# An einsum of attention weights and values: v through SyncE's queue in float32 with a cast on VectorE, and stores of four heads by SyncE

## The chip, the core and the metric

The kernel runs on one core of one Trainium2 chip. The core has TensorE (PE: matrix products, and transposes as products with an identity), VectorE (DVE), ScalarE (ACT), GpSimd (POOL) and SyncE (SP), each with its own instruction stream, and 16 DMA engines that move data between HBM and the core's on-chip memory (SBUF). DMAs issued by POOL stand in one queue (q0 in the profile), those issued by SP in another (q1); all 16 DMA engines serve both. Engines order themselves by semaphores: an instruction or a finished DMA raises one, another waits until it has reached a count; a DMA raises its semaphore by 16 in all. The metric is the device time of one execution in microseconds; lower is better.

## The reference

```python
attn_weights: (8, 12, 1024, 1024) float32
v:            (8, 12, 1024, 64)   float32
out = einsum('bhqs,bhsd->bhqd', attn_weights, v)      # float32
```

So there are 96 independent heads, and for each a product of a 1024x1024 matrix with a 1024x64 matrix. The weights are 402.7 MB, v and the output 25.2 MB each.

## The kernel before

**Tiling.** Four consecutive heads make a quad (`VH = 4`, `NV = 24` quads, called q). A quad is worked off in two units (`NU = 48` units, called n, so q = n // 2). The 128 partitions hold four heads by 32 blocks of rows. A unit takes 16 of the 32 rows of each block: `load_attn(n)` brings them as one DMA from POOL, cast by the DMA from float32 to bfloat16, into one of two buffers `abf[n % 2]` (64 KB read and 32 KB written for each partition). The last two units are loaded in two halves (`HALVED`).

**PE, one unit** (`pe_unit`). It waits for the load, transposes 16 groups g (four instructions each, line 132) into four PSUM banks in turn, from which DVE (10 groups) and ACT (6 groups) copy them to `at` (line 256, `copy_g`). In the first unit of a quad it then spreads v (line 147): v arrives as `vr`, two quads wide, in the layout of the DMA, and a product with a 0/1 matrix brings it to the partitions where the product needs it; DVE and ACT copy the result to `vbf` (line 232). Then it transposes the result of the unit before back (line 159), ACT copies that to the output buffer `osb` (line 239, `back_copies`), and PE multiplies (line 174). DVE and ACT each copy half of the product to `ot` (line 268, `product`), which releases the back transposes of the next unit.

**POOL** issues nearly all DMAs, in one written order. After the transposes of unit n (it waits for DVE's groups, `s_t[True]`) it issues load n + 2. In the first unit of an odd quad it first waits until the spread of that quad is done (`s_sp`) and issues the load of v for the next two quads (`load_v`, line 325): one DMA of 2 MB, cast by the DMA into `vr`. In the first unit of an even quad, after the load, it stores two finished quads (`store_2`, line 332, 2 MB). From quad 16 (`HELD_FROM`) on stores are held: quads 16 to 19 are stored by POOL after the last load, quads 20 to 23 by SP at the end.

**SP** loads the first two quads of v at the start, as float32, into `v32` (the last two slots of `osb`, which only the last two quads use for output), in four DMAs (line 385); DVE casts them to `vr` in one instruction (line 309). Then SP is a relay: it waits for each load in turn (line 396) and raises `s_half`, for which PE waits ahead of group 8; when a load of v has landed it raises `s_vr`, for which PE waits ahead of the spread; when a store has landed it raises `s_free`, for which ACT waits before it writes that slot of `osb` again. At load 35 it issues 15 tiny DMAs to `small`, a buffer that nothing reads (line 400): the k-th has k rows of k + 1 elements.

**Output slots.** `slot(q)` is q % 4 for quads 0 to 17, so four slots go round, and one slot each for the later quads.

Of the kernel before, what the change touches and what calls it, by code (L numbers as in the profile page):

```python
# [10 lines left out]
def kernel(  # L11
# [18 lines left out]
    nc = tc.nc  # L30
# [8 lines left out]
    VH = 4  # L39
    VP = P // VH  # L40
# [6 lines left out]
    NV = NH // VH  # L47
    NU = 2 * NV


    HELD_FROM = NV - 8
    BY_SYNC = NV - 4


    LOOPED = HELD_FROM
    NO = 8 + 2
    SMALL_AT = (33,)

    HALVED = NU - 2

    def slot(q):
# [4 lines left out]
    out_2 = out.rearrange("b h q d -> (b h) q d").rearrange(  # L66
        "(hq two four) (p r) d -> hq (four p) two (r d)", two=2, four=VH, p=VP
    )
    v_2 = v.rearrange("b h q d -> (b h) q d").rearrange(
        "(hq two four) (p r) d -> hq (four p) two (r d)", two=2, four=VH, p=VP  # L70
    )

    def on_dve(g):
        return g % 8 in (0, 2, 4, 5, 7)
# [8 lines left out]
    with tc.tile_critical(no_gpsimd_drain=True):  # L83
        sem = tc.alloc_semaphore
        sb = lambda name, shape, dt: nc.alloc_sbuf_tensor(name, shape, dt).ap()
        ident = sb("ident", [P, P], fp32)
# [5 lines left out]
        ot = sb("ot", [P, GH, P], fp32)  # L92
        osb = sb("osb", [P, NO, 2 * G, D], fp32)

        v32 = osb[:, ds(NO - 2, 2)].rearrange("p n r d -> p (n r d)")
        small = sb("small", [16, 2, 16, 16], fp32)
        bank = [nc.alloc_psum_tensor(f"bank{i}", [P, 512], fp32).ap() for i in range(8)]
        pt = [b.rearrange("p (k j) -> p k j", k=KW) for b in bank[:4]]
# [3 lines left out]

        s_abf = [sem(f"s_abf{i}") for i in range(2)]
        s_second = {n: sem(f"s_second{n}") for n in range(HALVED, NU)}
        s_v0, s_v = sem("s_v0"), sem("s_v")
        s_osb = [sem(f"s_osb{i}") for i in range(2)]
        s_held, s_end, s_small = sem("s_held"), sem("s_end"), sem("s_small")

        s_t = {True: sem("s_t_dve"), False: sem("s_t_act")}
# [114 lines left out]
        def engine(dve):  # L224
            eng = nc.vector if dve else nc.scalar
            copy = nc.vector.tensor_copy if dve else nc.scalar.copy
            per = PER_DVE if dve else PER_ACT
            e = 0 if dve else 1

            def spread_copy(h, ps, count):  # L230
                eng.wait_ge(s_sp[e], count)
                copy(  # L232
                    out=vbf[:, :, h], in_=ps.rearrange("p (k d) -> p k d", k=SB)
                ).then_inc(s_vbf[e])

            def back_copy(rows, j0, jn, ps, count):

                eng.wait_ge(s_back, count)
                return copy(  # L239
                    out=rows.rearrange("p (half j) d -> p j half d", half=2)[:, ds(j0, jn)],  # L240
                    in_=ps[:, ds(0, jn * P)].rearrange("p (j half d) -> p j half d", half=2, d=D),
                )

            def rows_of(n):
                return osb[:, slot(n // 2), ds(n % 2 * G, G)]

            def back_copies(rows, count, free=None):
                if free is not None:
                    eng.wait_ge(s_free, free)
                for k in range(2):  # L250
                    last = back_copy(rows, 4 * k, 4, px[k], count + k + 1)
                last.then_inc(s_out)

            def copy_g(g, count):
                eng.wait_ge(s_t[dve], count)  # L255
                ins = copy(  # L256
                    out=at[:, g].rearrange("c k j two -> c (k j two)"),
                    in_=bank[g % 4].bitcast(bf16),
                )
                if g < G - 4:  # L260
                    ins.then_inc(s_cp[g])
                elif g == (G - 1 if dve else G - 2):
                    ins.then_inc(s_last[e])

            def product(count):

                eng.wait_ge(s_m[e], count)
                copy(  # L268
                    out=ot.rearrange("c j (h p) -> c h j p", h=VH)[:, ds(2 * e, 2)],
                    in_=po[e].rearrange("c (h j p) -> c h j p", h=2, j=GH),  # L270
                ).then_inc(s_ot[e])

            mine = [g for g in range(G) if on_dve(g) == dve]

            def unit(n, base, rows, free):

                of_t, of_sp, of_back, of_m = base
                for g in mine:
                    copy_g(g, of_t + (n * per + count_of(g)))
                if n % 2 == 0:  # L280
                    spread_copy(e, po[e], of_sp + (n + 1))
                    spread_copy(2 + e, px[e], of_sp + (n + 2))
                if not dve:
                    back_copies(rows, of_back + 2 * n, free)
                product(of_m + (n + 1))


            un, iters = (2, NV) if dve else (8, LOOPED // 4)
            with nc.Fori(1, iters + 1, 1, engines=(DVE if dve else ACT,)) as it:  # L289
                base = [eng.snap(it * (un * k) - un * k) for k in (per, 1, 2, 1)]  # L290
                of_free = None if dve else eng.snap(it * 2 - 1)
                for n in range(un):
                    rows = osb[:, (n - 1) // 2 % 4, ds((n - 1) % 2 * G, G)]

                    free = of_free + n // 4 if n in (1, 5) and not dve else None
                    unit(n, base, rows, free)
            for n in range(un * iters, NU):
                free = LOOPED // 2 + 1 if n == un * iters + 1 else None
                unit(n, (0, 0, 0, 0), rows_of(n - 1), free)
            k = 1 - e  # L300
            back_copy(rows_of(NU - 1), 4 * k, 4, px[k], 2 * NU + k + 1).then_inc(s_fin[k])
# [3 lines left out]

        for h in range(2):
            nc.vector.memset(ot[:, :, ds(h * HP, HP)], 0.0).then_inc(s_ot[h])
        nc.vector.wait_ge(s_v0, 16 * 4)
        nc.vector.tensor_copy(out=vr.rearrange("p two b x -> p (two b x)"), in_=v32).then_inc(s_vr, 2)  # L309
        engine(True)  # L310
        engine(False)

# [8 lines left out]
                    in_=attn_q[n // 2][:, ds((n % 2 * G + g0) * S, gn * S)],  # L321
                ).then_inc(s_abf[n % 2] if g0 == 0 else s_second[n], 16)

        def load_v(iv):
            pool.dma_start(  # L325
                out=vr.rearrange("p two b x -> p two (b x)"), in_=v_2[iv]
            ).then_inc(s_v, 16)

        def store(q, fours, eng, done):
            eng.wait_ge(s_out, 2 * (q + fours) + 1)  # L330
            at_slot = osb[:, ds(slot(q), fours)].rearrange("p n r d -> p n (r d)")
            eng.dma_start(  # L332
                out=out_2[q // 2] if fours == 2 else out_q[q],
                in_=at_slot if fours == 2 else at_slot[:, 0],
                **({"single_packet": True} if eng is pool else {}),
            ).then_inc(done, 16)

        def store_2(q):
            store(q, 2, pool, s_osb[q // 2 % 2] if q < HELD_FROM else s_held)

        load_attn(0)
        load_attn(1)
# [20 lines left out]
                channel_multiplier=VB,  # L363
            ).then_inc(s_const)
        for n in range(NU - 2):
            q, i = n // 2, n % 2
            if i == 0 and q % 2 == 1 and q + 1 < NV:
                for s in s_sp:
                    pool.wait_ge(s, 2 * q + 2)
                load_v((q + 1) // 2)  # L370
            pool.wait_ge(s_t[True], (n + 1) * PER_DVE)
            load_attn(n + 2)
            if i == 0 and q % 2 == 0 and 0 < q <= HELD_FROM:
                store_2(q - 2)
        for q in range(HELD_FROM, BY_SYNC, 2):
            store_2(q)
        pool.drain()

        v32_2 = v32.rearrange("p (two x) -> p two x", two=2)
        for two, p0, pn in ((0, 0, P), (1, 0, 96), (1, 96, 22), (1, 118, 10)):
            nc.sync.dma_start(  # L385
                out=v32_2[ds(p0, pn), two], in_=v_2[0][ds(p0, pn), two]
            ).then_inc(s_v0, 16)
        nc.sync.sem_inc(s_free, 2)
        nc.sync.wait_ge(s_const, 1 + VH)
        for n in range(-2, NU - 2):  # L390

            if n + 2 < HALVED:
                nc.sync.wait_ge(s_abf[n % 2], 16 * ((n + 2) // 2 + 1))
            else:
                nc.sync.wait_ge(s_second[n + 2], 16)
            nc.sync.sem_inc(s_half)
            if n in SMALL_AT:

                for k in range(1, 16):
                    nc.sync.dma_start(  # L400
                        out=small[0:k, SMALL_AT.index(n), k, 0 : k + 1], in_=ident[0:k, 0 : k + 1]
                    ).then_inc(s_small, 16)
            if n >= 0 and n % 2 == 0:
                q = n // 2
                if q % 2 == 1 and q + 1 < NV:
                    nc.sync.wait_ge(s_v, 16 * ((q + 1) // 2))
                    nc.sync.sem_inc(s_vr, 2)
                if q % 2 == 1 and 1 < q <= HELD_FROM:
                    nc.sync.wait_ge(s_osb[(q - 3) // 2 % 2], 16 * ((q - 3) // 4 + 1))
                    nc.sync.sem_inc(s_free)  # L410
        store(NV - 4, 2, nc.sync, s_end)
        store(NV - 2, 1, nc.sync, s_end)
        rows = osb[:, slot(NV - 1)].rearrange("p (u half j) d -> p u half j d", u=2, half=2)
# [3 lines left out]
        for k in range(2):  # L417
            nc.sync.wait_ge(s_fin[k], 1)
            js = ds(4 * k, 4)
            nc.sync.dma_start(out=outs[:, 1, :, js], in_=rows[:, 1, :, js]).then_inc(s_end, 16)  # L420
        for k in range(2):
            nc.sync.wait_ge(s_osb[k], 16 * (HELD_FROM // 4))
        nc.sync.wait_ge(s_held, 16 * (BY_SYNC - HELD_FROM) // 2)
        nc.sync.wait_ge(s_end, 16 * 5)
        nc.sync.wait_ge(s_small, 16 * 15 * len(SMALL_AT))
# [30 lines left out]
```

## Time and profile before

| what | value |
|---|---|
| device time, median of 3 runs | 1055.34 us (1054.95 to 1055.54) |
| span of the profiled execution | 1052.9 us |
| loads of the weights by POOL, 4 MB written each | 46, and 4 of 2 MB |
| loads of v by POOL, 1 MB written each (2 MB read) | 11, 17.1 us to landing |
| stores by POOL, 2 MB each | 10, 29.5 us to landing |
| read from HBM, written to HBM | 427.8 MB, 25.2 MB |
| PE transposes (line 132), products (line 174) | 452.4 us, 215.0 us busy |

The table says how large each part is and not what sets the time. The page gives, besides busy times, the share of the span that the packets of each DMA queue fill on the 16 DMA engines, and the trace has a record of every DMA packet: its start, its queue, the bytes it wrote and how long it took, though not which of the 16 engines carried it. A packet is one row: 64 KB read and 32 KB written for a load of the weights, 8 KB read and 4 KB written for v cast by the DMA, 8 KB read and written for a store or for v in float32. A completion record of 4 bytes follows the last row of a DMA on each engine. In the timeline each line gives start, busy time, engine, line, operation, tiles, shapes and count, and in brackets the idle time before it and what ended it.

### The profile page before, as it was taken

How to read it: one execution, taken by the hardware profiler on the slowest of the kernel's cores; microseconds unless marked ns; L12 is line 12 of the kernel's file. 1: busy time of each engine (PE TensorE's matmuls, PEld its weight loads, DVE VectorE, ACT ScalarE, POOL GpSimd, SP SyncE). 2: the span in 40 equal slices, each digit the busy share in tenths (PEclk: the TensorE clock that was granted, in tenths of full speed). 3: DMA queues.
4: the chain of work that ended last, by engine and by line, in shares of the span. 5: the costliest groups of instructions: out<-in, count | busy, mean ns of one | idle time of the engine just before them, and what ended most of it. 6: DMA issues, size and time to landing. Idle time of an engine off the chain costs nothing.

```text
span 1052.9 us, 16298 instructions
## 1 busy us (share of the span) xinstructions
PE 736.3 (70%) x6920; PEld 690.5 (66%) x6920; DVE 388.5 (37%) x582; ACT 397.7 (38%) x485; POOL 45.0 (4%) x80
## 2 busy tenths in 40 slices
PE   0787676577696578767668757776776866875895
PEld 0776676576686568656668657665666766875884
DVE  0443344333353234333334324423333433532542
ACT  0443344333353334433344324433333433533452
POOL 1000000000000000000000000000000000000000
PEclk9989788898798888889889888888988987988898
DMA  9999999999999999999999999999999999999998
GB/s 236 223 220 211 215 255 215 219 218 247 231 210 253 218 217 259 219 217 228 241 215 217 257 219 218 258 214 218 248 222 218 218 208 228 218 206 226 210 218 339
DMA packets 14574, 240.21 MB, mean 228 GB/s; under 512 B 1511, under 2 KB 2023, under 8 KB 4967
## 3 DMA queue, kind: packets, MB, share of 16 engines
q0 software_dynamic: 12912, 233.84, 99.0%
q1 hardware_dynamic: 1655, 6.30, 1.6%
q8 instruction: 2, 0.03, 0.0%
q14 instruction: 5, 0.04, 0.0%
HBM read 427.82 MB, written 25.17 MB: 430 GB/s over the span
## 4 chain that ended last, share of the span: by engine, by line
DMA 75%; PE 22%; issue 1%; DVE 0%; SPq 0%; ACT 0%; POOL 0%; DVEq 0%
DMA abf<-in_attn_weights_dram 73%; PE bank L132 21%; DMA osb<-in_v_dram 3%; PE bank L174 1%; PE bank L159 0%; DVE vbf L232 0%; SPq L385 0%; PE bank L147 0%; DVE at L256 0%; DVE osb L239 0%; ACT ot L268 0%; POOL abf L319 0%; DVEq L255 0%; DVE vr L309 0%; DVEq L289 0%
## 5 line engine op out<-in xcount | busy, mean ns | idle before, releaser
L132 PE MATMUL bank<-ident,abf 128*128 128x128 f32 x3072 | 452.4, 318 | 274.8 <-DMA abf<-in_attn_weights_dram 269.4
L132 PEld LDWEIGHTS bank<-ident,abf 128*128 128x128 f32 x3072 | 442.5, 215 | 288.0 <-DMA abf<-in_attn_weights_dram 281.2
L256 DVE COPY at<-bank 128x1024 bf16<-128x1024 bf16 x480 | 320.0, 689 | 465.7 <-PE bank L132 462.9
L256 ACT COPY at<-bank 128x1024 bf16<-128x1024 bf16 x288 | 288.8, 1012 | 429.9 <-PE bank L132 429.9
L174 PE MATMUL bank<-at,vbf 128*64 128x256 bf16 x3072 | 215.0, 278 | 0.0
L174 PEld LDWEIGHTS bank<-at,vbf 128*64 128x64 bf16 x3072 | 196.8, 108 | 13.3 <-DVE at L256 4.0
L268 ACT COPY ot<-bank 128x512 f32<-128x512 f32 x48 | 28.1, 585 | 181.0 <-PE bank L174 181.0
L268 DVE COPY ot<-bank 128x512 f32<-128x512 f32 x48 | 33.2, 692 | 151.4 <-PE bank L174 151.4
L159 PE MATMUL bank<-ident,ot 128*128 128x128 f32 x392 | 52.2, 276 | 33.0 <-DVE vbf L232 32.2
L159 PEld LDWEIGHTS bank<-ident,ot 128*128 128x128 f32 x392 | 43.4, 141 | 45.1 <-DVE vbf L232 44.0
L239 ACT COPY osb<-bank 128x512 f32<-128x512 f32 x97 | 52.1, 589 | 22.5 <-PE bank L159 22.5
L319 POOL DMA_DIRECT2D abf<-in_attn_weights_dram x50 | 27.2, 545 | 694.1 <-PE bank L132 693.0
L232 DVE CAST vbf<-bank 128x512 bf16<-128x512 f32 x48 | 30.9, 686 | 6.5 <-PE bank L147 6.5
L232 ACT CAST vbf<-bank 128x512 bf16<-128x512 f32 x48 | 25.8, 589 | 11.9 <-PE bank L147 11.9
L147 PE MATMUL bank<-vr,spread 32*128 32x512 bf16 x384 | 25.7, 377 | 0.0
L325 POOL DMA_DIRECT2D vr<-in_v_dram x11 | 7.7, 703 | 236.1 <-PE bank L147 236.1
L147 PEld LDWEIGHTS bank<-vr,spread 32*128 32x128 bf16 x384 | 10.0, 93 | 6.9
L309 DVE CAST vr<-osb 128x4096 bf16<-128x4096 f32 x1 | 2.3, 2295 | 28.5 <-DMA osb<-in_v_dram 28.5
L332 POOL DMA_DIRECT2D out_dram<-osb x10 | 7.1, 715 | 28.6 <-ACT osb L239 28.6
L256 ACT ACT_TABLE_LOAD x4 | 5.1, 1283 | 1.1 <-SPq L83 1.1
L356 POOL TENSOR_SCALAR_AFFINE_SELECT spread<-spread 32x512 bf16<-32x512 bf16 x4 | 2.5, 628 | 0.6
L239 DVE COPY osb<-bank 128x512 f32<-128x512 f32 x1 | 0.7, 693 | 3.1 <-PE bank L159 3.1
(8 smaller groups left out, 2.1 us busy)
## 6 DMA issues: line engine op xcount, KB each, us to landing
abf<-in_attn_weights_dram POOLq DMA_DIRECT2D x46, 4096.0 KB, 33.5
out_dram<-osb POOLq DMA_DIRECT2D x10, 2048.0 KB, 29.5
vr<-in_v_dram POOLq DMA_DIRECT2D x11, 1024.0 KB, 17.1
abf<-in_attn_weights_dram POOLq DMA_DIRECT2D x4, 2048.0 KB, 24.0
out_dram<-osb SPq DMA_DIRECT2D x1, 2048.0 KB, 13.8
osb<-in_v_dram SPq DMA_DIRECT2D x1, 1024.0 KB
out_dram<-osb SPq DMA_DIRECT2D x1, 1024.0 KB, 15.9
osb<-in_v_dram SPq DMA_DIRECT2D x1, 768.0 KB
```

What stands on the lines that cost most here:

```text
L132: last = pe.matmul(out=pt[g % 4][:, k], lhsT=words[:, k], rhs=ident, is_transpose=True, start=(k == 0), stop=(k == KW - 1),)
L147: last = pe.matmul(out=ps, lhsT=spread[rows, b], rhs=vr[rows, two, b], start=(b == 0), stop=(b == VB - 1),)
L159: last = pe.matmul(out=ps[:, ds(j * P, P)], lhsT=ot[:, j0 + j], rhs=ident, is_transpose=True, start=(j == 0), stop=(j == jn - 1),)
L174: last = pe.matmul(out=outs, lhsT=vbf[:, 2 * kw + par, h], rhs=at[:, ds(half * GH, GH), kw, ds(h * VP, VP), par], start=(n == 0), stop=(n ...
L232: copy(out=vbf[:, :, h], in_=ps.rearrange("p (k d) -> p k d", k=SB)).then_inc(s_vbf[e])
L239: return copy(out=rows.rearrange("p (half j) d -> p j half d", half=2)[:, ds(j0, jn)], in_=ps[:, ds(0, jn * P)].rearrange("p (j half d) -> ...
L256: ins = copy(out=at[:, g].rearrange("c k j two -> c (k j two)"), in_=bank[g % 4].bitcast(bf16),)
L268: copy(out=ot.rearrange("c j (h p) -> c h j p", h=VH)[:, ds(2 * e, 2)], in_=po[e].rearrange("c (h j p) -> c h j p", h=2, j=GH),).then_inc( ...
L319: pool.dma_start(out=abf[n % 2][:, ds(g0, gn)].rearrange("p g s -> p (g s)"), in_=attn_q[n // 2][:, ds((n % 2 * G + g0) * S, gn * S)],).th ...
L325: pool.dma_start(out=vr.rearrange("p two b x -> p two (b x)"), in_=v_2[iv]).then_inc(s_v, 16)
L332: eng.dma_start(out=out_2[q // 2] if fours == 2 else out_q[q], in_=at_slot if fours == 2 else at_slot[:, 0], **({"single_packet": True} if ...
L356: pool.affine_select(out=spread[ds(h * VP, VP)], in_=spread[ds(h * VP, VP)], compare_op=mybir.AluOpType.not_equal, fill=1.0, base=0, patte ...
```

## The change

All loads of v go through SP's queue, as float32 and one quad (1 MB) at a time, into the two halves of `v32`; DVE casts each quad to `vr`. Stores of quads 0 to 15 go through SP's queue too, one quad (1 MB) at a time, with one semaphore for each of the four slots (`RING`). POOL's loop is left with the loads of the weights; the held stores of quads 16 to 19 stay with it. The relay of loads by SP goes: `s_half` is raised for all units but the last two at the start. The 15 tiny DMAs are issued by SP after it has issued the load of v for quad 20.

```diff
-    SMALL_AT = (33,)
+    RING = 4
+    SMALL_AT = (HELD_FROM,)
...
+            def cast_v(two):
+                return nc.vector.tensor_copy(
+                    out=vr[:, two].rearrange("p b x -> p (b x)"), in_=v32[:, two]
+                ).then_inc(s_vr)
...
                 if not dve:
                     back_copies(rows, of_back + 2 * n, free)
+                if of_v is not None and n % 2 == 1:
+                    eng.wait_ge(s_v[n // 2], of_v)
+                    cast_v(n // 2)
                 product(of_m + (n + 1))
...
+            if dve:
+                for two, count in ((0, 1), (1, 3)):
+                    nc.vector.wait_ge(s_v0[two], 16 * count)
+                    cast_v(two)
-            un, iters = (2, NV) if dve else (8, LOOPED // 4)
+            un, iters = (4, NV // 2 - 1) if dve else (2 * RING, LOOPED // RING)
...
-        nc.vector.wait_ge(s_v0, 16 * 4)
-        nc.vector.tensor_copy(out=vr.rearrange("p two b x -> p (two b x)"), in_=v32).then_inc(s_vr, 2)
...
-        def load_v(iv):
-            pool.dma_start(
-                out=vr.rearrange("p two b x -> p two (b x)"), in_=v_2[iv]
-            ).then_inc(s_v, 16)
...
         for n in range(NU - 2):
-            q, i = n // 2, n % 2
-            if i == 0 and q % 2 == 1 and q + 1 < NV:
-                for s in s_sp:
-                    pool.wait_ge(s, 2 * q + 2)
-                load_v((q + 1) // 2)
             pool.wait_ge(s_t[True], (n + 1) * PER_DVE)
             load_attn(n + 2)
-            if i == 0 and q % 2 == 0 and 0 < q <= HELD_FROM:
-                store_2(q - 2)
...
-        nc.sync.sem_inc(s_free, 2)
+        nc.sync.sem_inc(s_half, HALVED)
+        nc.sync.sem_inc(s_free, RING)
         nc.sync.wait_ge(s_const, 1 + VH)
-        for n in range(-2, NU - 2):
-            if n + 2 < HALVED:
-                nc.sync.wait_ge(s_abf[n % 2], 16 * ((n + 2) // 2 + 1))
-            else:
-                nc.sync.wait_ge(s_second[n + 2], 16)
-            nc.sync.sem_inc(s_half)
...
+        def load_v(q):
+            nc.sync.wait_ge(s_vr, q - 1)
+            nc.sync.dma_start(out=v32[:, q % 2], in_=v_q[q]).then_inc(s_v[q % 2], 16)
+
+        load_v(2)
+        load_v(3)
+        for q in range(BY_SYNC):
+            if q + 4 < NV:
+                load_v(q + 4)
+            if q < HELD_FROM:
+                store(q, 1, nc.sync, s_osb[q % RING])
+            if 0 <= q - 2 < HELD_FROM + 2 - RING:
+                nc.sync.wait_ge(s_osb[(q - 2) % RING], 16 * ((q - 2) // RING + 1))
+                nc.sync.sem_inc(s_free)
+            if q in SMALL_AT:
...
+        for n in range(HALVED, NU):
+            nc.sync.wait_ge(s_second[n], 16)
+            nc.sync.sem_inc(s_half)
```

More of the change, by code (lines that the diff above doesn't have):

```diff
@@ L68 @@
     )
-    v_2 = v.rearrange("b h q d -> (b h) q d").rearrange(
-        "(hq two four) (p r) d -> hq (four p) two (r d)", two=2, four=VH, p=VP
-    )
+    v_q = v.rearrange("b (hq four) (p r) d -> (b hq) (four p) (r d)", four=VH, p=VP)
     def on_dve(g):
@@ L93 @@
         osb = sb("osb", [P, NO, 2 * G, D], fp32)
-        v32 = osb[:, ds(NO - 2, 2)].rearrange("p n r d -> p (n r d)")
+        v32 = osb[:, ds(NO - 2, 2)].rearrange("p n r d -> p n (r d)")
         small = sb("small", [16, 2, 16, 16], fp32)
@@ L104 @@
         s_second = {n: sem(f"s_second{n}") for n in range(HALVED, NU)}
-        s_v0, s_v = sem("s_v0"), sem("s_v")
-        s_osb = [sem(f"s_osb{i}") for i in range(2)]
+        s_v0, s_v = [sem(f"s_v0_{i}") for i in range(2)], [sem(f"s_v_{i}") for i in range(2)]
+        s_osb = [sem(f"s_osb{i}") for i in range(RING)]
         s_held, s_end, s_small = sem("s_held"), sem("s_end"), sem("s_small")
@@ L273, in engine, with unit @@
             mine = [g for g in range(G) if on_dve(g) == dve]
-            def unit(n, base, rows, free):
+            def cast_v(two):
+                return nc.vector.tensor_copy(
+                    out=vr[:, two].rearrange("p b x -> p (b x)"), in_=v32[:, two]
+                ).then_inc(s_vr)
+            def unit(n, base, rows, free, of_v=None):
                 of_t, of_sp, of_back, of_m = base
@@ L284, in unit @@
                     back_copies(rows, of_back + 2 * n, free)
+                if of_v is not None and n % 2 == 1:
+                    eng.wait_ge(s_v[n // 2], of_v)
+                    cast_v(n // 2)
                 product(of_m + (n + 1))
-            un, iters = (2, NV) if dve else (8, LOOPED // 4)
+            if dve:
[3 more added lines that the diff above has]
+            un, iters = (4, NV // 2 - 1) if dve else (2 * RING, LOOPED // RING)
             with nc.Fori(1, iters + 1, 1, engines=(DVE if dve else ACT,)) as it:
                 base = [eng.snap(it * (un * k) - un * k) for k in (per, 1, 2, 1)]
-                of_free = None if dve else eng.snap(it * 2 - 1)
+                of_free = None if dve else eng.snap(it * RING - (RING - 1))
+                of_v = eng.snap(it * 16) if dve else None
                 for n in range(un):
                     rows = osb[:, (n - 1) // 2 % 4, ds((n - 1) % 2 * G, G)]
-                    free = of_free + n // 4 if n in (1, 5) and not dve else None
-                    unit(n, base, rows, free)
+                    free = of_free + n // 2 if n % 2 == 1 and not dve else None
+                    unit(n, base, rows, free, of_v)
             for n in range(un * iters, NU):
-                free = LOOPED // 2 + 1 if n == un * iters + 1 else None
+                free = n // 2 + 1 if n in (2 * LOOPED + 1, 2 * LOOPED + 3) else None
                 unit(n, (0, 0, 0, 0), rows_of(n - 1), free)
@@ L336, in store @@
             ).then_inc(done, 16)
-        def store_2(q):
-            store(q, 2, pool, s_osb[q // 2 % 2] if q < HELD_FROM else s_held)
         load_attn(0)
@@ L365 @@
         for n in range(NU - 2):
-            q, i = n // 2, n % 2
-            if i == 0 and q % 2 == 1 and q + 1 < NV:
-                for s in s_sp:
-                    pool.wait_ge(s, 2 * q + 2)
-                load_v((q + 1) // 2)
             pool.wait_ge(s_t[True], (n + 1) * PER_DVE)
             load_attn(n + 2)
-            if i == 0 and q % 2 == 0 and 0 < q <= HELD_FROM:
-                store_2(q - 2)
         for q in range(HELD_FROM, BY_SYNC, 2):
-            store_2(q)
+            store(q, 2, pool, s_held)
@@ L377 @@
         pool.drain()
-        v32_2 = v32.rearrange("p (two x) -> p two x", two=2)
         for two, p0, pn in ((0, 0, P), (1, 0, 96), (1, 96, 22), (1, 118, 10)):
-            nc.sync.dma_start(
-                out=v32_2[ds(p0, pn), two], in_=v_2[0][ds(p0, pn), two]
-            ).then_inc(s_v0, 16)
-        nc.sync.sem_inc(s_free, 2)
-        nc.sync.wait_ge(s_const, 1 + VH)
-        for n in range(-2, NU - 2):
-            if n + 2 < HALVED:
-                nc.sync.wait_ge(s_abf[n % 2], 16 * ((n + 2) // 2 + 1))
-            else:
-                nc.sync.wait_ge(s_second[n + 2], 16)
-            nc.sync.sem_inc(s_half)
-            if n in SMALL_AT:
+            nc.sync.dma_start(out=v32[ds(p0, pn), two], in_=v_q[two][ds(p0, pn)]).then_inc(
+                s_v0[two], 16
+            )
@@ L399 @@
                 for k in range(1, 16):
                     nc.sync.dma_start(
-                        out=small[0:k, SMALL_AT.index(n), k, 0 : k + 1], in_=ident[0:k, 0 : k + 1]
+                        out=small[0:k, SMALL_AT.index(q), k, 0 : k + 1], in_=ident[0:k, 0 : k + 1]
                     ).then_inc(s_small, 16)
[L403 to L410, printed above, removed]
+        for n in range(HALVED, NU):
+            nc.sync.wait_ge(s_second[n], 16)
+            nc.sync.sem_inc(s_half)
@@ L420 @@
             nc.sync.dma_start(out=outs[:, 1, :, js], in_=rows[:, 1, :, js]).then_inc(s_end, 16)
-        for k in range(2):
-            nc.sync.wait_ge(s_osb[k], 16 * (HELD_FROM // 4))
+        for k in range(RING):
+            nc.sync.wait_ge(s_osb[k], 16 * (HELD_FROM // RING))
         nc.sync.wait_ge(s_held, 16 * (BY_SYNC - HELD_FROM) // 2)
```

## The prediction

> **What bounds the kernel now.** I read the page's first three parts, then the chain that ended last in order of time, then the timeline of one late unit, then the records of single DMA packets.
>
> ```profile
> span 1052.9 us, 16298 instructions
> PE 736.3 (70%) x6920; PEld 690.5 (66%) x6920; DVE 388.5 (37%) x582; ACT 397.7 (38%) x485; POOL 45.0 (4%) x80
> ...
> DMA  9999999999999999999999999999999999999998
> ...
> q0 software_dynamic: 12912, 233.84, 99.0%
> q1 hardware_dynamic: 1655, 6.30, 1.6%
> ...
> DMA 75%; PE 22%; issue 1%; DVE 0%; SPq 0%; ACT 0%; POOL 0%; DVEq 0%
> ```
>
> No engine is near full, but packets fill the 16 DMA engines for 99.0% + 1.6% of the span (records overlap a little at their ends, hence over 100%). The chain looks like a ping-pong of loads and transposes; one late unit shows that it is not one:
>
> ```profile
> 866.79 9.47 PE L132 MATMUL bank<-ident,abf 128*128 128x128 f32 x64 [2.29 <-DMA abf<-in_attn_weights_dram]
> ...
> 876.30 0.69 DVE L256 COPY at<-bank 128x1024 bf16<-128x1024 bf16 x1 [0.16 <-PE bank L132]
> 876.57 0.53 POOL L319 DMA_DIRECT2D abf<-in_attn_weights_dram  x1 [16.96 <-PE bank L132]
> 876.74 1.07 ACT L239 COPY osb<-bank 128x512 f32<-128x512 f32 x2
> 877.07 4.21 PEld L174 LDWEIGHTS bank<-at,vbf 128*64 128x64 bf16 x64 [0.17 <-DVE at L256]
> 877.07 4.48 PE L174 MATMUL bank<-at,vbf 128*64 128x256 bf16 x64
> 879.64 0.69 DVE L268 COPY ot<-bank 128x512 f32<-128x512 f32 x1 [2.65 <-PE bank L174]
> 881.58 0.58 ACT L268 COPY ot<-bank 128x512 f32<-128x512 f32 x1 [3.77 <-PE bank L174]
> 891.04 9.08 PEld L132 LDWEIGHTS bank<-ident,abf 128*128 128x128 f32 x62 [9.77 <-DMA abf<-in_attn_weights_dram]
> ```
>
> Load 41 is issued at 876.57, while load 40 is still arriving (its transposes start at 891.04): the queue holds some 14 us of work at each issue, and PE then waits 9.8 us. So **the time is the work of the DMA engines**, and it can be counted from the packet records. They name no engine, but each packet starts where another ended, so one engine can be followed (start us, queue, KB written, took ns):
>
> ```
> 40.222  q0 32 2432    42.635  q0 32 2432    45.048  q0 32 2431    loads back to back: 2413 ns apart
> 786.448 q0  4  324    786.753 q0  4  324    787.057 q0  4  324    v, cast by the DMA: 304.7 ns apart
> 149.069 q0  8  309    149.375 q0  8  309    149.681 q0  8  309    stores in q0: 306 ns apart
> 8.275   q0 32 2431    10.687  q1  8  322    11.006  q0 32 2431    13.417 q1 8 322   load and v by SP: 2730.7 ns a pair
> ```
>
> A load is 8 packets an engine, v of four heads 8, a store of four heads 8. Bill of one engine up to the last load: 46 loads x (8 x 2412.8 + 21 for the completion record) = 888.9 us; halved loads 32 x 1208.5 ns = 38.7; v by Pool 11 x (16 x 304.7 + 21) = 53.9; first v 16 x 306 = 4.9; eight stores x (16 x 306 + 13 + 8) = 39.3. Sum 1025.7, with the first packet at 2.0 us, 1027.7; the records show the last load's packets ending at about 1029.5, and the packets between 2 and 1031 us leave only 0.6 us an engine uncovered. **There is no idle DMA time to win**; the rest is the tail (about 21 us from there).
>
> **The change, part by part.** Sums are differences on the profiled span of 1052.9 us; the median of the runs, 1055.34, lies 2.4 us above it, and I add the difference to the median.
>
> *Bytes.* Each v byte is read once as float32 before and after; only the written side doubles. The packets say that this costs nothing by itself: 8 KB read and 4 KB written takes 304.7 ns, 8 KB read and written 306. 22 x 8 packets x 1 ns = +0.2 us.
>
> *Two queues instead of one.* Before, v and the stores stand in q0 as runs of 16 rows between loads. After, they stand in SP's q1 beside a q0 that is never empty. The start of before shows what follows (last line of the packet table): the engine takes one 64 KB row of a load, one 8 KB row of q1, in turn, and the 8 KB row then adds 2730.7 - 2412.8 = 318 ns, not 306. The same 319 ns is in the first row of a store run that follows a load in q0 and in no later row of it, so it belongs to the change from a casting to a plain packet. In the tail, where q0 and q1 both store, rows alternate at 306: alternating alone is free. Before pays it 8 times (store runs), after on nearly every row: 38 transfers (v 22, stores 16) x (8 x 318 + 4 for the completion in q1) = 96.8 us, for 53.9 + 39.3 = 93.2 us before: **+3.6 us**. At the end of each load q0's completion record takes a turn, and the q1 row after it costs 306 and the record 18 instead of 21: some 42 loads x 15 ns = **-0.6 us**.
>
> The Trainium skill (DMA: Bandwidth & Descriptors, Queues, rings and completion order) says that an engine drains a whole packet of some 9 to 17 descriptors from one queue before it turns to the next. The start of before disagrees: one 8 KB row a turn. By that rule the 8 rows of a transfer would go in one run, and the sum would be -0.2 us in place of +3.0; this is the second rival below.
>
> *Deadlines of v.* One load and one 1 MB q1 transfer take 8 x 2730.7 + 22 = 21.9 us together, and each two units bring two loads, one v and one store: q1's demand just matches its turns. From 8 us on q1 always has something, so a v lands some 45 us after its issue; it is issued four units (87 us) before its cast. No wait. Stores have a ring of four, 174 us.
>
> *The cast on DVE.* One cast of 128x2048 is half of this row, 1.15 us, 22 times in odd units:
>
> ```profile
> L309 DVE CAST vr<-osb 128x4096 bf16<-128x4096 f32 x1 | 2.3, 2295 | 28.5 <-DMA osb<-in_v_dram 28.5
> ```
>
> It stands ahead of the product copy, behind which DVE's next copies queue; DVE waits there 2.65 us for PE (line at 879.64). 1.15 us goes into that: 0. Without the cover it would be 25 us of DVE, which PE's 9.8 us of waiting a unit would still hide.
>
> *Pool* loses 11 x 703 and 8 x 712 ns of issues and its waits for the spread; loads are issued up to 3 us sooner into a queue that is not empty: 0. *SP* gains 36 issues of 0.39 to 0.48 us and loses the relay, in which PE waited only in the last two units; those stay. *Start*: the first cast is split, DVE begins its copies 1.1 us earlier; the DMA engines are busy then: 0.
>
> *The 15 tiny transfers.*
>
> ```profile
> 784.61 11.30 SPq L400 DMA_DIRECT2D small<-ident  x15
> ```
>
> One engine gets 30 turns of q1 from them, 788.6 to 849.4 us in the records. In after they go out about 33 us earlier, and v of quad 21 now queues behind them: 793 (end of quad 20's v) + 61 to 73 + 22 = 876 to 888 us. Its cast is due at about 880. DVE may stand 8 us; the next load lands at 891 or later, so that is covered too: 0.
>
> *What the trace does not show*: stores row by row between loads. When all engines turned to a store at once, packets of loads in flight were stretched by 40 to 960 ns (around 146, 320 and 408 us; the bursts at 235, 497 and 758 show next to none): all stretches from 6 us on add up to 0.85 us an engine. Lower bound: they vanish, -0.85. Upper: each of an engine's 128 store rows stretches a load by 0.85 us / 8 bursts = 0.1 us at most: +13 us, half of it likelier as the bound, since the late bursts, whose engines were spread over 1 us and more, show none. I take 0, as the late bursts are nearest to the new case.
>
> Sum: 3.6 - 0.6 = **+3.0 us: 1058.3 us**, +0.29%. What a measurement here can tell from no change is about 0.2%, 2.1 us.
>
> **Rivals.**
> 1. *No change* (not slower): the rows of one q1 transfer go in a run, or the 12 ns belong to the start alone. The place is the turn of the DMA engine, the price 304 rows x 12 ns; it decides once fewer than three rows in four pay the 12 ns. For it: the page's rule; also the Trainium skill (same page, Issuing engines are not separate DMA queues) that another issuing engine only saves issue time. Against: 16 engines alternating by single rows from 8 to 27 us. 1055.34 - 0.2 = 1055.1 us, with vanished stretches 1054.3.
> 2. *Stores disturb loads*: +3.0 and a stretch of 50 ns on each of 128 store rows, +6.4: 1064.7 us. For it the early bursts, against it the late ones.
> 3. *v of quad 21 comes late*: decides once it lands after about 901 (the 891 at which PE wants DVE, and the 10 us for which the queue still holds a load). It needs 13 us more backlog in q1 than counted; each further us is a us of idle engines. 5 us: 1063 us. Against: q1's demand matches its turns, it doesn't grow.
> 4. *Faster by more than 2.1 us*: only if DMA work disappears; 0.6 uncovered and 0.85 stretched are all that the records offer.
>
> **How the numbers follow.** Forecast 0.50 (1056.8 to 1060; 0.07 of it lies under the bound of 1057.45), no change 0.23, stores disturb 0.15, late v 0.07, faster 0.05. Slower 0.43 + 0.15 + 0.07 = 0.65, same 0.07 + 0.23 = 0.30, faster 0.05. The range takes the no-change case down to its 1054.5 and most of the stretch up to 1064.
>
> **What would show it.** In the profile of the changed kernel: q1's share near 1.6 + 9.2%, q0's near 90%; packets of 8 KB in q1 at 322 ns, singly between loads; DMA full in all slices; casts of 1.15 us with DVE's wait before L267 shorter by that; the last load landing 3 us later. Wrong would be: runs of q1 rows at 306 ns; load packets well over 2432 ns all along; DVE waiting for v before a cast; PE waiting for DVE near 890 us.

## The result and the profile after

| | kernel before | changed kernel |
|---|---|---|
| device time, median of 18 runs each | 1055.02 us (1053.94 to 1055.56) | 1056.61 us (1056.21 to 1057.38) |
| ratio, with its 95% interval | | 1.0015 (1.0009 to 1.0022) |
| span of the profiled execution | 1052.9 us | 1054.7 us |

The change makes the kernel slower by 1.6 us, 0.15%: the interval leaves out no change, but the difference is under the 0.2% that the prediction had set as its bound. The forecast was +3.0 us, so the direction was right, the time lies in the range, and the size was about half. The time is 0.2 us under the band of 1056.8 to 1060 us to which the prediction gave 0.50; counted from the prediction's own start, 1055.34 + 1.6 = 1056.9 us, it is just inside.

The page of the changed kernel, its first three parts:

```profile
span 1054.7 us, 16257 instructions
PE 749.0 (71%) x6920; PEld 703.6 (67%) x6920; DVE 413.9 (39%) x605; ACT 398.1 (38%) x485; POOL 31.1 (3%) x61
...
DMA  9999999999999999999999999999999999999998
...
q0 software_dynamic: 7744, 205.52, 89.6%
q1 hardware_dynamic: 7127, 46.15, 10.8%
```

The DMA engines are as full as before: what left q0 stands in q1 now, 10.8% of the span where the prediction said 1.6 + 9.2%. DVE has 25 us more work and nobody waits for it: PE's waits for DVE's copies of v (`vbf`) come to 32.2 us in both kernels. The same unit as before, in the timeline of the changed kernel:

```profile
885.25 0.53 POOL L329 DMA_DIRECT2D abf<-in_attn_weights_dram  x1 [20.40 <-PE bank L131]
885.42 1.07 ACT L238 COPY osb<-bank 128x512 f32<-128x512 f32 x2
885.60 1.22 DVE L275 CAST vr<-osb 128x2048 bf16<-128x2048 f32 x1
885.75 4.21 PEld L173 LDWEIGHTS bank<-at,vbf 128*64 128x64 bf16 x64 [0.17 <-DVE at L255]
885.75 4.48 PE L173 MATMUL bank<-at,vbf 128*64 128x256 bf16 x64
886.84 0.33 SPq L389 DMA_DIRECT2D osb<-in_v_dram  x1
888.33 0.69 DVE L267 COPY ot<-bank 128x512 f32<-128x512 f32 x1 [1.52 <-PE bank L173]
890.27 0.58 ACT L267 COPY ot<-bank 128x512 f32<-128x512 f32 x1 [3.77 <-PE bank L173]
895.73 9.30 PEld L131 LDWEIGHTS bank<-ident,abf 128*128 128x128 f32 x64 [5.77 <-DMA abf<-in_attn_weights_dram]
```

The cast (885.60, 1.22 us) has gone into DVE's wait ahead of the product copy, which is 1.52 us now and was 2.65, and SP issues the next v as soon as the cast is over. PE still waits for the load.

So the time has to be in the packets. One engine of the changed kernel, followed in the packet records (start us, queue, KB written, distance to the next in ns; "rec" is a completion record):

```
300.506 q0 32 2412   302.918 q1 8 319   303.237 q0 32 2412   305.649 q1 8 319   305.968 q0 32 2411   308.379 q1 8 319
308.698 q0 32 2412   311.110 q1 8 319   311.429 q0 rec 6     311.435 q1 rec 5   311.440 q0 32 2412   313.852 q1 8 319
```

This is the picture foretold: one row of a load, one row of SP's queue, each of the latter at 319 ns (the prediction's 322 is the length of the record, which overlaps the next by 3). The bill between 32 and 1028 us, as a mean over the 16 engines, from the records' durations less their overlap with the next:

| | before | changed | difference |
|---|---|---|---|
| v and stores, 304 rows | 53.7 + 39.2 = 92.9 us | 301.6 rows in 95.9; 304 would be 96.6 | +3.7 us |
| completion records | 1.2 | 0.7 | -0.5 |
| rows of loads, ns each; 368 rows | 2414.3 | 2411.9 | -0.9 us |
| sum | | | +2.3 us |
| last load's rows end, mean of the engines | 1029.85 us | 1032.07 us | +2.2 us |
| last load's rows end, slowest | 1031.08 us | 1032.89 us | +1.8 us |

From the last load on both kernels take the same 21.8 us to the end of the span (1052.9 - 1031.1, 1054.7 - 1032.9).

### The profile page after: what moved, and what is told of

Its sections match the earlier page's. It is cut to its first block, busy times and chain, and to the rows that moved or that the text cites. A ratio compares the mean times of both kernels' runs of the same rounds, so it can differ in the third digit from the quotient of the medians.

```text
span 1054.7 us, 16257 instructions
## 1 busy us (share of the span) xinstructions
PE 749.0 (71%) x6920; PEld 703.6 (67%) x6920; DVE 413.9 (39%) x605; ACT 398.1 (38%) x485; POOL 31.1 (3%) x61
## 3 DMA queue, kind: packets, MB, share of 16 engines
q1 hardware_dynamic: 7127, 46.15, 10.8%
## 4 chain that ended last, share of the span: by engine, by line
DMA 76%; PE 22%; issue 1%; POOL 0%; DVE 0%; ACT 0%; POOLq 0%; SPq 0%
DMA abf<-in_attn_weights_dram 76%; PE bank L131 22%; PE bank L173 0%; PE bank L158 0%; POOL abf L329 0%; DVE osb L238 0%; ACT ot L267 0%; POOLq L450 0%; SPq L409 0%; SPq L82 0%
## 5 line engine op out<-in xcount | busy, mean ns | idle before, releaser
L131 PE MATMUL bank<-ident,abf 128*128 128x128 f32 x3072 | 465.1, 324 | 265.1 <-DMA abf<-in_attn_weights_dram 260.9
L131 PEld LDWEIGHTS bank<-ident,abf 128*128 128x128 f32 x3072 | 455.6, 215 | 278.0 <-DMA abf<-in_attn_weights_dram 273.0
L158 PE MATMUL bank<-ident,ot 128*128 128x128 f32 x392 | 52.2, 276 | 33.0 <-DVE vbf L231 32.2
L275 DVE CAST vr<-osb 128x2048 bf16<-128x2048 f32 x24 | 29.3, 1220 | 26.8 <-DMA osb<-in_v_dram 26.8
L337 POOL DMA_DIRECT2D out_dram<-osb x2 | 1.4, 724 | 0.0
```

The lines of the kernel that those rows point to most:

```text
L131: last = pe.matmul(out=pt[g % 4][:, k], lhsT=words[:, k], rhs=ident, is_transpose=True, start=(k == 0), stop=(k == KW - 1),)
L158: last = pe.matmul(out=ps[:, ds(j * P, P)], lhsT=ot[:, j0 + j], rhs=ident, is_transpose=True, start=(j == 0), stop=(j == jn - 1),)
L275: return nc.vector.tensor_copy(out=vr[:, two].rearrange("p b x -> p (b x)"), in_=v32[:, two]).then_inc(s_vr)
L337: eng.dma_start(out=out_2[q // 2] if fours == 2 else out_q[q], in_=at_slot if fours == 2 else at_slot[:, 0], **({"single_packet": True} if ...
```

## The experiments

All times are medians on the same chip as the runs of the kernel before that stand beside them. "Mean end" is the mean over the engines of the end of the last load's rows: 1029.85 us in the kernel before.

**The same transfers in one queue.** v in float32, the cast on DVE and the quad-wise transfers stay; v and the stores are issued by POOL, behind its loads. SP only keeps the release of the slots and the tiny DMAs.

```diff
         for n in range(NU - 2):
             pool.wait_ge(s_t[True], (n + 1) * PER_DVE)
             load_attn(n + 2)
+            if n % 2 == 0 and 0 < n and n // 2 + 3 < NV:
+                load_v(n // 2 + 3)
+            if n % 2 == 1 and 0 <= (n - 3) // 2 < HELD_FROM:
+                store((n - 3) // 2, 1, pool, s_osb[(n - 3) // 2 % RING])
...
```

> As the changed kernel (v in float32, cast on DVE, one quad a transfer, stores of one quad), but v and the stores stand in POOL's queue behind the loads, not in SP's. Theory (the cost is the alternation: every plain 8 KB row that follows a load row costs 319 ns, not 306): rows go in runs of 8 again, 319 once and 306 seven times, so an engine pays 22 x (13 + 8 x 306 + 21) = 54.6 us for v and 16 x (13 + 8 x 306 + 8) = 39.5 for the stores, +0.9 us on the kernel before, 2.7 less than SP's queue by the same count; time +0.3 to +1.0 us on before. Rival (the cost is what DVE, the quad-wise transfers or the new waits do, not the queue): as the changed kernel, +1.6 us, and last load landing as late as there.

Measured: 1054.98 us against 1055.01 before, ratio 0.9999 (0.9990 to 1.0008); mean end 1030.33 us. The loss is gone with the second queue alone; that DVE casts, that the transfers are quad-wise and that SP no longer relays cost nothing that can be measured. The theory's +0.3 to +1.0 us is not seen in the time, but the interval reaches +0.8, and the mean end is 0.5 us later. Its page and one of its engines:

```profile
span 1053.6 us, 16259 instructions
...
q0 software_dynamic: 13216, 245.37, 98.8%
q1 hardware_dynamic: 1655, 6.30, 1.5%
```

```
303.437 q0 32 2413   305.850 q0 rec 3   305.853 q0 8 319   306.172 q0 8 306   306.478 q0 8 306   306.784 q0 8 306   ...   308.313 q0 rec 9
```

One row at 319 and the rest at 306: the prediction's reading, that the 12 to 13 ns belong to a plain row that follows a casting one, holds within one queue as well.

**One packet by a mark.** POOL's stores carry a mark that they be one packet; here SP's v and stores get it too.

```diff
-                **({"single_packet": True} if eng is pool else {}),
+                single_packet=True,
...
-            nc.sync.dma_start(out=v32[:, q % 2], in_=v_q[q]).then_inc(s_v[q % 2], 16)
+            nc.sync.dma_start(out=v32[:, q % 2], in_=v_q[q], single_packet=True).then_inc(s_v[q % 2], 16)
```

> The changed kernel, with v's loads and the stores of SP's queue marked as one packet each (as POOL's stores already are). Theory: an engine turns between queues at packets, and unmarked rows are a packet each; marked, the 8 rows of a transfer go in one turn: 319 once, 306 seven times, 304 rows less 266 x 12.5 ns = 3.3 us of DMA work an engine gone, time -1.5 us to +0.3 us on the kernel before, so 1.5 to 3 us under the changed kernel. Rival: the mark changes nothing in SP's queue or the rows alternate anyway: +1.6 us on before, rows at 322 ns singly between loads.

Measured: 1056.66 us, ratio 1.0015 (1.0006 to 1.0024), mean end 1032.02. The theory's half on the mark was wrong, the rival was right: rows go singly between loads at 319 ns as in the changed kernel. SP's queue can't be made to send runs this way.

**Each half of the change alone.** First the stores in SP's queue and v with POOL as before; then v in SP's queue, with the cast, and the stores with POOL as before.

```diff
 (stores only, against the changed kernel)
...
-        load_v(2)
-        load_v(3)
-        for q in range(BY_SYNC):
-            if q + 4 < NV:
-                load_v(q + 4)
+        for q in range(NV):
+            if q % 2 == 1 and q + 1 < NV:
+                nc.sync.wait_ge(s_v, 16 * ((q + 1) // 2))
+                nc.sync.sem_inc(s_vr, 2)
             if q < HELD_FROM:
                 store(q, 1, nc.sync, s_osb[q % RING])
 (v only, against the changed kernel: POOL's loop, then SP's)
             load_attn(n + 2)
+            if n % 4 == 0 and 0 < n // 2 <= HELD_FROM:
+                store(n // 2 - 2, 2, pool, s_osb[(n // 2 - 2) // 2 % 2])
...
-            if q < HELD_FROM:
-                store(q, 1, nc.sync, s_osb[q % RING])
...
```

> Only the stores of quads 0 to 15 go to SP's queue, one quad each; v stays cast by POOL's DMA, two quads at a time. Theory: 128 store rows alternate with load rows: 16 x (8 x 318 + 4) = 40.8 for 39.3 us, +1.5, less 0.25 for the loads' completion records and up to 0.5 for stretched packets that vanish: +0.7 to +1.3 us on before; store rows at 322 ns. Rival one (v and its cast are the whole cost): 0. Rival two (stores row by row disturb the loads): load packets well over 2432 ns, +4 us and more.

> Only v goes to SP's queue in float32 with the cast on DVE; stores stay with POOL, two quads at a time. Theory: 176 v rows alternate with load rows: 22 x (8 x 318 + 4) = 56.1 for 53.9 us, +2.2, less 0.35 for the loads' completion records: +1.5 to +2.0 us on before; the stretched load packets at the start of store bursts stay. Rival (the stores in SP's queue are the cost): 0.

Measured: stores only 1056.28 us, ratio 1.0013 (1.0004 to 1.0022), mean end 1030.89 (+1.0); v only 1056.88, ratio 1.0016 (1.0007 to 1.0025), mean end 1032.04 (+2.2). Both as the theory had it; stores among loads don't stretch them lastingly. But the halves add up to 3.2 us of mean end and the whole is 2.2. The stretched load rows account for nearly all of that: 0.58 us an engine in the kernel before, 0.79 with the stores alone, 0.76 with v alone, 1.02 with everything in POOL's queue, 0.04 with both in SP's queue. In the five kernels whose POOL queue holds bursts of v or stores between loads, some load rows are stretched where many engines leave their loads at the same moment; in the kernels without such bursts next to none are. (With the stores alone it is one event, around 80 us, where the first v and the first store come together.) What the stretching itself is, no run here shows.

The kernel with v alone in SP's queue also shows what alternation costs where both rows are plain. Here q1 brings v while q0 is in a burst of stores:

```
329.749 q0 8 306   330.055 q1 8 306   330.361 q0 8 305   330.666 q1 8 306   330.972 q0 8 306   331.278 q1 8 306
```

Turning between queues is free here (306 ns, as within one queue); turning from a casting row to a plain one costs 12 to 13 ns (319 ns).

**Twice the rows.** The stores-only kernel, each store cut into two DMAs of 4 KB rows.

```diff
...
-                store(q, 1, nc.sync, s_osb[q % RING])
+                nc.sync.wait_ge(s_out, 2 * (q + 1) + 1)
+                for u in range(2):
+                    nc.sync.dma_start(
+                        out=out_q[q][:, ds(u * G * D, G * D)],
+                        in_=osb[:, slot(q), ds(u * G, G)].rearrange("p r d -> p (r d)"),
+                    ).then_inc(s_osb[q % RING], 16)
...
```

> As the kernel in which only the stores go to SP's queue (+1.27 us on before), but each store of a quad is two DMAs of 4 KB rows: twice the rows, the same bytes. Theory (a fixed cost for each plain row behind a casting row): a 4 KB row alone is 153 to 155 ns apart, with 12.5 ns 166 to 168, so a store costs 16 x 167 + 8 = 2.68 us an engine for 2.55: 16 x 0.13 = +2.0 us on that kernel, +2.7 to +3.7 us on before; rows of 4 KB at 172 ns. Rival (a cost by byte or by transfer): +1.3 to +1.5 us on before, rows at 159 ns.

Measured: 1057.40 us against 1055.28 before, ratio 1.0021 (1.0012 to 1.0030); mean end 1032.61, 1.7 us after the stores-only kernel for the expected 2.0; its stretched rows come to 0.44 us in place of 0.79, which is the rest. The time, +2.1 us, misses the 2.7 to 3.7 expected, and its interval (+1.3 to +3.2) reaches both that and the rival's +1.3 to +1.5: the time alone decides nothing. The packets do, and they are as the theory had them: 172 ns long, 168 to 169 from start to start. The bytes are the same, so the cost doesn't go by bytes. The edit doubles the DMAs as well as the rows; that the price is a row's and not a DMA's is seen in the packets, where single rows pay it.

**The changed kernel again, and two parts of it.** Four casts in place of one (three into a buffer that nothing reads); and the tiny DMAs left out.

```diff
 (four casts)
             def cast_v(two, again=0):
+                for x in range(again):
+                    nc.vector.tensor_copy(out=extra[:, x], in_=v32[:, two])
...
-                    cast_v(n // 2)
+                    cast_v(n // 2, 3)
 (no tiny DMAs)
-    SMALL_AT = (HELD_FROM,)
+    SMALL_AT = ()
...
```

> The changed kernel once more, beside the three that follow: +1.6 us on the kernel before (+0.8 to +2.4). A second trace of it, to tell what belongs to one execution: 8 KB rows of SP's queue at 322 ns again, load packets of 32 KB hardly stretched (under 0.1 us an engine from 32 us on, where the kernel before had 0.58).

> The changed kernel with each of the 22 casts in the loop done four times (three of them into a buffer that nothing reads): DVE gets 22 x 3 x 1.22 = 80 us more, and its product copy in odd units comes some 2.3 us later, since the cast filled only 1.2 of its 2.65 us of waiting. Theory (DMA engines bound, DVE covered): as the changed kernel, within 0.5 us. Rival (the cast is what costs): +1.6 us becomes +5 to +6.5 us on before.

> The changed kernel without the 15 tiny DMAs, whose 30 turns on one engine stand ahead of v of quad 21. Theory (v comes in time anyway): as the changed kernel, within 0.5 us; v of quad 21 lands some 40 to 60 us sooner after its issue. Rival (the late v costs): 1 us or more under the changed kernel.

Measured, against 1055.28 before: the changed kernel 1056.63 us, ratio 1.0012 (1.0003 to 1.0021), mean end 1031.84, stretched rows 0.02 us; four casts 1056.69, ratio 1.0014 (1.0005 to 1.0023); no tiny DMAs 1056.99, ratio 1.0015 (1.0006 to 1.0025). Four casts change nothing (+0.1 us). Without the tiny DMAs the kernel is 0.4 us later and not sooner, within the 0.5 allowed; the runs don't show why. In the waits and groups of the kernel with four casts

```profile
L277 DVE CAST extra<-osb 128x2048 bf16<-128x2048 f32 x66 | 76.7, 1218 | 0.0
...
L268 DVE COPY ot<-bank 128x512 f32<-128x512 f32 x48 | 32.9, 686 | 93.0 <-PE bank L174 93.0
```

DVE's wait ahead of the product copy is 93.0 us in all, in 26 of the 48 units; in the 22 units with a cast there is none left; the 77 us more are hidden all the same, since PE has its wait for loads to give. The tiny DMAs do hold v of quad 21 up. Shortest, median and longest time to landing over all DMAs of `osb`, first the changed kernel, then without them:

```profile
DMA to landing us min/median/max: 4.5/32.6/75.7
```

```profile
DMA to landing us min/median/max: 5.3/32.0/45.2
```

The 75.7 is v of quad 21, issued at 804.7 us and landed at about 880. Without the tiny DMAs the longest is another transfer's: this v, issued at 805.6, has its last completion record at 830.7, after 25 us. So it lands 50 us sooner after its issue, in the 40 to 60 expected. It makes no difference, since in the changed kernel its cast starts at 885.60 straight behind DVE's last copy, as the unit above shows: it was in time by some 5 us.

## Why the prediction was nearly right, and where its size was off

- *The bound.* Right: full DMA engines before and after, and the time follows the last load's rows in every kernel: each span ends 21.8 to 22.3 us after the slowest engine's last row.
- *Two queues.* Right in mechanism and close in size: 3.6 - 0.6 = +3.0 us foretold, 3.7 - 0.5 = +3.2 counted for rows and records. The two splits are not the same: of the 15 ns a load behind the foretold -0.6, 12 are rows behind a completion record, which the count has among the rows; and the foretold 318 ns a row has in it the nanosecond by which the load row ahead is shorter, 0.3 us in all, which the count has among the loads. In the prediction's terms that is +2.9 for +3.0. Taking the second queue away gives the loss back (0.9999), and twice the rows pay twice in the packets.
- *The step that was mis-sized* is the stretching of loads by stores. The prediction gave -0.85 (they vanish) to +13 us and took 0, because the late bursts of stores were "nearest to the new case". They showed next to no stretching; if the new case was like them, the stretches of the early bursts had to vanish, so the value to take was near the lower end. From 32 us on they fell from 0.58 to 0.04 us an engine (the 0.85 counts from 6 us on, and what lies in the first loads stays). With the nanosecond a row named above, loads gave back 0.9 us. That makes +2.3 us of DMA work for the +3.0.
- *A term that was not in the sum*: the end hangs on the slowest engine, not on the mean. It was 1.2 us behind the mean before and 0.8 us after, which takes another 0.4 us off. One trace each; the second trace of the changed kernel has 0.6, so this part may be chance.
- *Deadlines.* No wait for v after the first two casts, as foretold, and stores never held up ACT. The time to landing was foretold at some 45 us; it is less, since q1 does empty at times:

```profile
DVE vr L275 <- DMA osb<-in_v_dram: 26.8, 2, 23.4
```

```profile
osb<-in_v_dram SPq DMA_DIRECT2D x23, 1024.0 KB, 33.6
out_dram<-osb SPq DMA_DIRECT2D x17, 1024.0 KB, 31.0
```

  The first line is from the waits (us in total, times, longest): two, both at the start. The others are from the DMA issues (the last column is the median from issue to landing).
- *The cast, POOL, the start, the tail*: nothing seen, as foretold; a cast took 1.22 us for the 1.15, and four cost nothing either. The 9.8 us of PE's waiting "a unit" was that of one unit; the mean of its waits for loads was 281.2 / 45 = 6.2 us, still more than a cast.
- *Rivals.* No change at all is ruled out by the interval, though the loss is too small for the 0.2% set as the bound, and 0.65 had been put on more than that. Stores that disturb loads: wrong sign (0.58 us of stretching before, 0.04 after). Late v: landed some 5 us ahead of its cast. The rule of the Trainium skill (DMA: Bandwidth & Descriptors, Queues, rings and completion order), a whole packet of several descriptors a turn, did not hold for SP's queue even with the one-packet mark: single rows, 319 ns each. The prediction calls it its second rival; it belongs to the first of its list, no change.

## What to carry to other kernels

When the profile shows the DMA engines full, count the packets: a transfer's cost is its rows times their spacing, and that depends on what runs next to them on the same engine. Here a second queue beside one that never empties added no bandwidth; it mixed the two row by row. With the plain rows together behind casting loads, in one queue, the price (319 ns for 306) was paid once a run instead of once a row. Against that, the mix had no bursts, and load rows that had been stretched around bursts came back to their plain length.

## What was not expected of the hardware

- A plain 8 KB row costs 306 ns behind another plain row, from either queue, and 319 behind a load row that is cast on the way (start to start); the records of plain 4 KB rows are 159 ns long behind a plain row and 172 behind such a load. A v row that is cast itself does not pay it (304.7 ns).
- A completion record in between changes nothing in that. Load, record, plain row: 3 ns and 319 (305.850 and 305.853 us in the kernel with everything in POOL's queue). Plain row, record, plain row: 6 ns and 306 (312.943 and 312.949 us in the changed kernel).
- A completion record of a load takes 21 ns when the next row of a load stands behind it in its own queue, and 3 to 6 when the other queue has the next turn: 1.2 us an engine for all records before, 0.7 after, with more records.
- Marking SP's transfers as one packet did not change the order of rows: 1056.66 us, the same alternation.
